# Layer B's products of 128 columns in its first two groups as one product of whole F32 operands

## The chip, the cores and the metric

The kernel runs on one core of a Trainium2 chip. The metric is the time of one execution on the device in microseconds; a kernel's time is the median of several runs.

## The reference, cut to what matters

A decoder trunk of two layers on 1024 tokens of width 1024. Layer A is an mLSTM mixer, which the change leaves alone. Layer B is dilated sliding-window attention: 8 heads of width 128 and three groups with dilations 1, 4 and 16. In each group the tokens of one residue form a sequence that is cut into blocks of 128, and a query block sees its own block and the one before:

```python
GROUPS_B = ((128, 1), (512, 4), (2048, 16))
sc = jnp.einsum('nbqhd,nbkhd->nbhqk', qb, kb) * HEAD_DIM_B ** -0.5
sc = jnp.where(valid, sc + bias, -jnp.inf)
m = sc.max(-1)
e = jnp.exp(sc - m[..., None])
den = e.sum(-1)
o = jnp.einsum('nbhqk,nbkhd->nbqhd', e, vb) / den
```

With dilation 1 there is one sequence of eight blocks, with dilation 4 there are four of two blocks, with dilation 16 sixteen sequences of 64. A first block has no block before it, so its scores have 128 columns of keys; all others have 256. The three groups' outputs are then merged by their softmax denominators, gated, and projected.

## The kernel before

**Products in parts.** TensorE multiplies most matrices as F32R, a shorter form of F32. To keep the accuracy a matrix is held as a high and a low part (`split`: ScalarE's L92 casts to the high part, L93, mostly on VectorE, subtracts to get the low one), and `mm3` makes three products of them: high by high (L97), high by low (L98) and low by high (L99). L97 and L98 have the same stationary operand. In layer B's third group (dilation 16, `g == 2`) the scores (L1136) and the values' products (L1202) instead take whole F32 operands of 128 x 128 in one product.

**Layer B.** Heads are taken in two quads of four (`quad`), and in each quad group after group (`g` = 0, 1, 2), and in a group head after head. For each quad and group `values` first makes the values of four heads; then for each head `queries_keys` makes queries and keys by seven products of half-matrices (Strassen's scheme, `strassen_steps`, banks 0 to 3, products of 512 columns; the weights are loaded by L177, subtracted and added by L243 to L261, split at L92 and L93), `scores` makes eight score blocks with their row maxima (L1142, L1144) and exponentials (L1146), and `attend` transposes the probabilities on TensorE (L1159), splits them and multiplies them with the values (`av`).

**Blocks of 128 columns.** In `scores` of group 2 (dilation 4, `g == 1`) the even blocks, four a head, have 128 columns; in group 1 it is the first block alone. In `attend` two blocks of one key block are joined to 256 columns, and three products a head in group 1, four in group 2, are left with 128.

**Where the whole matrices come from.** `done` in `queries_keys` reads a quarter of queries (`i` = 0) or keys (`i` = 1) and writes its high part (ScalarE, L1095) and its low part (VectorE, L1096). Even blocks of group 2 lie in the quarters with `half == 0`.

**Residual blocks.** `residual(tb)`, called after each head of quad 0's second group, brings one block of 128 tokens of layer A's output up to date: a load (L989), a multiplication and an addition on VectorE (L845, L846) and a store (L991), all in slot 52.

**The order.** The program is recorded in the order of the code; a scheduler then sets the order of each engine's queue and of SP's queue, which issues all DMAs. Each queue runs strictly in that order. A slot (tile `s...`) or PSUM bank (`b...`) is written anew only after its last reader. Slots 38 and 39 hold the weights' quarters, slots 32 to 35 the four values' tiles; banks 4 and 5 take scores and transposes in turn, 6 and 7 the outputs. The values' weights of a next group land in part in two of the values' tiles of the group before.

## Time and profile before

| | |
|---|---|
| median of 3 runs | 2071.47 us (2068.67 to 2078.06) |
| the profiled execution's own time | 2070.5 us |
| its span | 2068.7 us |
| TensorE busy | 2001.8 us, 97% |
| VectorE busy | 1462.1 us, 71% |
| ScalarE busy | 1003.1 us, 48% |

Engines in the profile: PE is TensorE, PEld its loads of the stationary operand, DVE VectorE, ACT ScalarE, SP the queue that issues DMAs. Times are us, in groups the mean of one instruction is in ns. Records of TensorE overlap: a product's record lasts longer than the distance to the next one's start. A row of the timeline gives the start, the duration, the engine, the line, the operation, what it writes and reads, the shape and how many instructions the row joins; in brackets the engine's idle time before it and what ended it. A 128x512 product has 512 columns.

### The profile page before, as it was taken

The numbers are of one execution on the slowest core, as the hardware profiler recorded it, in microseconds if no ns is written. First come the engines' busy times: TensorE is split into PE (matmuls) and PEld (weight loads), VectorE is DVE, ScalarE is ACT, GpSimd is POOL, SyncE is SP. The second block draws the span as 40 slices with busy tenths as digits, with TensorE's granted clock in tenths as the row PEclk, the third lists the DMA queues.
The fourth block names the chain that finished last, engine by engine and source line by source line (L and its number), as shares of the span: only waits on it lengthen the run. The fifth ranks groups of instructions, "written<-read, shape, count | busy, mean of one in ns | idle before, by whom it ended". The sixth has DMA issues, their size and how long they took to land.

```text
span 2068.7 us, 29452 instructions
## 1 busy us (share of the span) xinstructions
PE 2001.8 (97%) x11008; PEld 1721.8 (83%) x11008; DVE 1462.1 (71%) x2825; ACT 1003.1 (48%) x1920; POOL 188.9 (9%) x145
## 2 busy tenths in 40 slices
PE   8989999999999999999999999999999999999997
PEld 6868888899888888877788898888888898888786
DVE  8787788465367767465678757766878757757878
ACT  5455555533745453343434536555534635655631
POOL 0230000600244443000000000000000000000000
PEclk9999999999999999999999999999999999999999
DMA  4455555443844643516113231122543132123753
GB/s 166 145 190 175 181 214 175 153 146 114 324 172 158 214 146 114 199 62 213 56 46 127 68 133 62 61 93 91 187 166 121 64 113 70 62 92 106 260 210 122
DMA packets 117046, 288.20 MB, mean 139 GB/s; under 512 B 13028, under 2 KB 43172, under 8 KB 116904
## 3 DMA queue, kind: packets, MB, share of 16 engines
q1 hardware_dynamic: 116904, 286.34, 39.2%
q8 instruction: 86, 1.41, 0.3%
q14 instruction: 56, 0.46, 0.1%
HBM read 200.00 MB, written 86.30 MB: 138 GB/s over the span
## 4 chain that ended last, share of the span: by engine, by line
PE 77%; DVE 11%; DMA 7%; ACT 2%; issue 2%; SPq 0%; DVEq 0%; ACTq 0%
PE b L97 24%; PE b L99 24%; PE b L98 24%; DVE s L93 3%; DMA s<-df 3%; PE b L521 1%; PE b L1159 1%; DMA s<-dv 1%; DVE s L141 1%; ACT s L92 1%; PE b L527 1%; PE b L788 1%; DVE s L1276 1%; DVE s L486 1%; DVE s L230 0%
## 5 line engine op out<-in xcount | busy, mean ns | idle before, releaser
L97 PE MATMUL b<-s,s 128*128 128x512 f32 (+2 forms) x3256 | 1125.4, 354 | 28.4 <-ACT s L92 16.7
L98 PE MATMUL b<-s,s 128*128 128x512 f32 (+2 forms) x3256 | 1140.6, 352 | 9.3 <-DVE s L93 9.3
L99 PE MATMUL b<-s,s 128*128 128x512 f32 (+2 forms) x3256 | 1125.1, 352 | 5.3 <-DVE s L93 5.1
L97 PEld LDWEIGHTS b<-s,s 128*128 128x128 f32 x3256 | 617.0, 190 | 117.4 <-ACT s L92 22.3
L92 ACT CAST s<-s 128x512 fp32r<-128x512 f32 (+4 forms) x674 | 435.1, 659 | 552.9 <-PE b L99 318.3
L98 PEld LDWEIGHTS b<-s,s 128*128 128x128 f32 x3256 | 619.7, 190 | 88.1 <-DVE s L93 10.7
L99 PEld LDWEIGHTS b<-s,s 128*128 128x128 f32 x3256 | 617.9, 190 | 88.5 <-DVE s L93 8.4
L93 DVE TENSOR_TENSOR s<-s,s 128x512 fp32r<-128x512 f32 (+3 forms) x656 | 500.9, 773 | 248.0 <-ACT s L92 245.4
L230 DVE TENSOR_TENSOR s<-s,b 128x512 f32<-128x512 f32 x192 | 130.5, 682 | 70.8 <-PE b L99 61.5
L224 DVE TENSOR_TENSOR s<-s,b 128x512 f32<-128x512 f32 x128 | 86.5, 680 | 26.6 <-PE b L99 25.9
L1146 ACT ACTIVATE s<-s,nmax 128x128 f32<-128x128 f32 (+1 forms) x192 | 84.5, 442 | 38.3 <-DVE nmax L1144 37.5
L93 DVE TENSOR_TENSOR s<-b,s 128x512 fp32r<-128x512 f32 (+1 forms) x96 | 59.0, 630 | 43.3 <-ACT s L92 43.0
L486 DVE SCALAR_TENSOR_TENSOR s<-s,c_convw,s 128x512 f32<-128x512 f32 (+3 forms) x96 | 74.8, 786 | 2.3 <-ACT s L483 1.8
L1142 DVE CUSTOM_DVE_ANT_0 s<-b,k 128x128 f32<-128x128 f32 (+1 forms) x192 | 57.8, 345 | 17.5 <-PE b L99 17.4
L243 DVE TENSOR_TENSOR s<-s,s 128x512 f32<-128x512 f32 (+1 forms) x55 | 41.6, 756 | 39.3 <-DMA s<-in_w_xm 13.9
L722 ACT ACTIVATE s<-s,k 128x128 f32<-128x128 f32 x144 | 46.9, 392 | 41.7 <-DVE s L93 19.3
L92 ACT CAST s<-b 128x512 fp32r<-128x512 f32 (+1 forms) x96 | 50.3, 545 | 31.8 <-PE b L99 19.7
L681 POOL TENSOR_TENSOR s<-s 128x512 fp32r<-128x512 f32 x32 | 43.3, 1369 | 161.6 <-DMA s<-dv 112.4
L93 POOL TENSOR_TENSOR s<-s,s 128x512 fp32r<-128x512 f32 x18 | 30.5, 1702 | 254.1 <-ACT s L92 253.2
L237 ACT COPY s<-b 128x512 f32<-128x512 f32 x64 | 37.4, 585 | 26.0 <-PE b L99 25.6
L792 POOL TENSOR_TENSOR s<-s,s 128x512 f32<-128x512 f32 x32 | 42.3, 1338 | 62.8 <-DVE s L791 47.9
L1095 ACT ACTIVATE s<-s 128x512 fp32r<-128x512 f32 x48 | 42.0, 882 | 11.8 <-DVE s L230 11.6
(178 smaller groups left out, 1448.4 us busy)
## 6 DMA issues: line engine op xcount, KB each, us to landing
s<-in_w_qk SPq DMA_DIRECT2D x48, 512.0 KB
s<-in_w_out SPq DMA_DIRECT2D x40, 512.0 KB
dp<-s SPq DMA_DIRECT2D x32, 512.0 KB
s<-dp SPq DMA_DIRECT2D x32, 512.0 KB
s<-in_w_z SPq DMA_DIRECT2D x24, 512.0 KB
s<-in_w_v SPq DMA_DIRECT2D x24, 512.0 KB
dg<-s SPq DMA_DIRECT2D x24, 512.0 KB
s<-dg SPq DMA_DIRECT2D x24, 512.0 KB
```

The lines of the kernel that those rows point to most:

```text
L92: self.nc.scalar.copy(h, src)
L93: (l_eng or self.nc.vector).tensor_tensor(l, src, f(h), op=ALU.subtract)
L97: mm(ps, lh, rh, start=start, stop=False, skip_group_check=skip)
L98: mm(ps, lh, rl, start=False, stop=False, skip_group_check=skip)
L99: mm(ps, ll, rh, start=False, stop=stop, skip_group_check=skip)
L224: V.tensor_tensor(o, p, q, op=add)
L230: V.tensor_tensor(o, p[lane][rows], q[lane][rows], op=add)
L486: V.scalar_tensor_tensor(u[i][:, lo:o + 512], xm[i][:, lo - s:o + 512 - s], convw[:, c, 3 - s:4 - s], u[i][:, lo:o + 512], op0=ALU.mult, o ...
L681: G.tensor_tensor(l, f(l), f(h), op=ALU.subtract)
L722: A.activation(E[:, i * P:i * P + P], src[:, i * P:i * P + P], AF.Exp, bias=self.bias[:, hd, ig, j:j + 1])
L1142: V.tensor_tensor_reduce(out=dst, in0=sc, in1=bias, op0=ALU.add, op1=ALU.max, scale=1.0, scalar=-3e38, accum_out=mx[:, b:b + 1])
L1146: A.activation(res[b][0], res[b][0], AF.Exp, bias=nm[:, b:b + 1], accum_out=stat[:, 1, g, b:b + 1])
```

## The change

In group 2 the four even blocks' scores, and in groups 1 and 2 the values' products of 128 columns, take whole F32 operands in one product.

- `queries_keys` in group 2 writes whole queries and keys of the even blocks into a new tile in slot 52 (L1099 of the new file). The queries of these blocks are no longer split, since nothing else reads them; the keys are split as well, since the odd blocks read them.
- `transposed` splits only the columns that 256-column products read; the rest of its bank goes to a new small tile `pw` (two buffers) by one ScalarE copy (L1181).
- `head_values` also hands out the values unsplit, straight from the values' tiles, and `av_whole` (L1193) multiplies them with `pw`; the new scores line is L1145.

```diff
@@ head_values, queries_keys
-            return [(h[:, at(b)[0], at(b)[1]], l[:, at(b)[0], at(b)[1]]) for b in range(8)]
+            whole = lambda half, t: v[half][i].rearrange("p (t n) -> p t n", t=4)[:, t, cs]
+            return [(h[:, at(b)[0], at(b)[1]], l[:, at(b)[0], at(b)[1]], whole(*at(b))) for b in range(8)]
...
+            whole = self.slot(52, (P, 2, 4, P)) if g == 1 else None
...
+                if g == 1 and half == 0:
+
+                    A.activation(whole[:, i], sv, AF.Copy, scale=scale)
+                    if i == 0:
+                        return
                 A.activation(dh, sv, AF.Copy, scale=scale)
                 V.scalar_tensor_tensor(dl, sv, scale, f(dh), op0=ALU.mult, op1=ALU.subtract)
@@ scores
+                    elif g == 1 and b % 2 == 0:
+                        T.matmul(ps[:, o:o + w], whole[:, 0, b // 2], whole[:, 1, b // 2], start=True, stop=True,
+                                 skip_group_check=True)
                     else:
                         self.mm3(ps[:, o:o + w], qh[:, bs], ql[:, bs], kh[:, ks], kl[:, ks], True, True, skip=True)
@@ attend
-                    self.split(ph[:, 0:n], pl[:, 0:n], pt[:, 0:n])
+                    m = n - P * n_whole
+                    self.split(ph[:, 0:m], pl[:, 0:m], pt[:, 0:m])
+                    if n_whole:
+                        pw = self.t(cp, [P, 2, P], tag="pw", bufs=2)
+                        A.copy(pw[:, 0:n_whole].rearrange("p j n -> p (j n)"), pt[:, m:n])
+                        return ph, pl, pw
...
+            def av_whole(bank, o, kb, p2, j, start):
+
+                T.matmul(po[bank][:, o:o + P], v[kb][2], p2[2][:, j], start=start, stop=True,
+                         skip_group_check=True)
...
-                    p2 = transposed(q0, q1[:, 0:P], q1[:, P:256])
+                    p2 = transposed(q0, q1[:, 0:P], q1[:, P:256], n_whole=1)
                     at = 256 * (r % 2)
-                    av(r // 2, at, 256, 2 * r, p2, 0, r % 2 == 0)
-                    av(r // 2, at + P, P, 2 * r + 1, p2, 256, False)
+                    av(r // 2, at, 2 * r, p2, 0, r % 2 == 0)
+                    av_whole(r // 2, at + P, 2 * r + 1, p2, 0, False)
```

The change also moves instructions, since the scheduler orders the new program anew. TensorE, where head 0's last outputs of group 2 (`b_1761`, in the new file `b_1770`) meet head 1's first scores (`b_1794`, `b_1808`). Before:

```order
L97 MATMUL b_1761_11368<-s_1769_11412,s_1758_11361 128x256
L98 MATMUL b_1761_11368<-s_1769_11412,s_1758_11361 128x256
L99 MATMUL b_1761_11368<-s_1769_11412,s_1759_11362 128x256
L97 MATMUL b_1761_11368<-s_1769_11412,s_1758_11361 128x128
L98 MATMUL b_1761_11368<-s_1769_11412,s_1758_11361 128x128
L99 MATMUL b_1761_11368<-s_1769_11412,s_1759_11362 128x128
L97 MATMUL b_1794_11571<-s_1773_11431,s_1772_11430 128x128
L98 MATMUL b_1794_11571<-s_1775_11433,s_1772_11430 128x128
L99 MATMUL b_1794_11571<-s_1773_11431,s_1774_11432 128x128
L97 MATMUL b_1794_11571<-s_1773_11431,s_1772_11430 128x256
```

and now (`pw` the copied probabilities, `s_1789` the whole queries and keys in slot 52):

```order
L1193 MATMUL b_1770_11353<-pw_11387,s_1736_11100 128x128
L97 MATMUL b_1770_11353<-s_1781_11397,s_1767_11346 128x256
L1145 MATMUL b_1808_11557<-s_1789_11419 128x128
L98 MATMUL b_1770_11353<-s_1781_11397,s_1767_11346 128x256
L99 MATMUL b_1770_11353<-s_1781_11397,s_1768_11347 128x256
L1193 MATMUL b_1770_11353<-pw_11400,s_1736_11100 128x128
L97 MATMUL b_1808_11557<-s_1786_11416,s_1785_11415 128x256
```

Each run of three 128-column products is one product there, and whole products stand between parts of 256 columns. SP's queue, at the start of quad 0's first group, where head 1's weights of queries and keys (`in_w_qk`) are issued (`dx` is the stored output of layer A, `dz` a gate). Before:

```order
L989 DMA s_1771_11425<-dx_77_142 128x1024
L1307 DMA dz_89_154<-s_1484_9208 128x512
L991 DMA dx_77_142<-s_1771_11425 128x1024
L989 DMA s_1811_11683<-dx_78_143 128x1024
L177 DMA s_1587_9973<-in_w_qk 128x1024
L177 DMA s_1588_9975<-in_w_qk 128x1024
L991 DMA dx_78_143<-s_1811_11683 128x1024
```

and now:

```order
L1329 DMA dz_89_154<-s_1484_9208 128x512
L177 DMA s_1589_9971<-in_w_qk 128x1024
L177 DMA s_1590_9973<-in_w_qk 128x1024
L177 DMA s_1630_10228<-in_w_qk 128x1024
L177 DMA s_1631_10230<-in_w_qk 128x1024
```

The residual blocks' loads and stores have left this place. They stand now in the second group, here after head 0's scores there (SP's queue; `s_1784` and `s_1829` are slot 52, `s_1835` and `s_1836` head 2's weights, `s_1881` and `s_1880` head 3's):

```order
L177 DMA s_1835_11671<-in_w_qk 128x1024
L989 DMA s_1784_11410<-dx_77_142 128x1024
L177 DMA s_1836_11673<-in_w_qk 128x1024
L991 DMA dx_77_142<-s_1784_11410 128x1024
L1234 DMA dg_84_149<-s_1783_11406 128x1024
L989 DMA s_1829_11661<-dx_78_143 128x1024
L177 DMA s_1881_11924<-in_w_qk 128x1024
```

One residual block follows each head's scores, and the next head's whole queries and keys can be written only after its store. On ScalarE the write (L1099) stands now among these:

```order
L92 CAST s_1778_11384<-b_1777_11380 128x256
L1099 ACTIVATE s_1789_11419<-b_1792_11424 128x512
L1232 COPY s_1783_11406<-b_1769_11352 128x2x256
L1099 ACTIVATE s_1789_11419<-s_1796_11428 128x512
L1102 ACTIVATE s_1786_11416<-s_1796_11428 128x4x128
L92 CAST s_1781_11397<-b_1780_11393 128x256
L1181 COPY pw_11387<-b_1777_11380 128x128
```

The first L1099 there is the one that waits for the residual block's store; what is below it in the list waits with it.

## Rows read from the trace of the kernel before

**Rows 1.** The page: busy time of each engine; the chain's share by engine.

```profile
PE 2001.8 (97%) x11008; PEld 1721.8 (83%) x11008; DVE 1462.1 (71%) x2825; ACT 1003.1 (48%) x1920; POOL 188.9 (9%) x145
...
PE 77%; DVE 11%; DMA 7%; ACT 2%; issue 2%; SPq 0%; DVEq 0%; ACTq 0%
```

**Rows 2.** Busy time by stretch: length, then PE, PEld, DVE, ACT, POOL; clock, DMA.

```profile
1295.00:1322.00 27.00, 27.00 (x150) 23.34 (x149) 20.77 (x49) 16.67 (x36) 0.00 (x0) 1.00 0.16 59
```

**Rows 3.** Groups by line and shape, layer B: count, busy us, mean ns, idle before.

```profile
L99 PE MATMUL b<-s,s 128*128 128x128 f32 x96 | 25.9, 274 | 0.0
...
L1136 PE MATMUL b<-s,s 128*128 128x128 f32 x128 | 17.0, 290 | 2.0 <-ACT s L1091 2.0
L1202 PE MATMUL b<-s,s 128*128 128x128 f32 x128 | 16.8, 274 | 0.0
```

**Rows 4.** Timeline of PE: scores of a head of group 2.

```profile
1341.75 0.22 PE L97 MATMUL b<-s,s 128*128 128x128 f32 x1
1341.81 0.28 PE L98 MATMUL b<-s,s 128*128 128x128 f32 x1
1341.92 0.27 PE L99 MATMUL b<-s,s 128*128 128x128 f32 x1
1342.03 0.33 PE L97 MATMUL b<-s,s 128*128 128x256 f32 x1
...
1342.43 0.22 PE L97 MATMUL b<-s,s 128*128 128x128 f32 x1
...
1343.01 0.52 PE L99 MATMUL b<-s,s 128*128 128x256 f32 x2
```

**Rows 5.** Timeline of PE: a run of 256-column parts; whole products of group 3.

```profile
1185.26 0.28 PE L98 MATMUL b<-s,s 128*128 128x256 f32 x1
...
1186.94 0.22 PE L97 MATMUL b<-s,s 128*128 128x128 f32 x1
...
1417.77 0.39 PE L97 MATMUL b<-s,s 128*128 128x512 f32 x1
1418.00 1.95 PE L1136 MATMUL b<-s,s 128*128 128x128 f32 x16
...
1420.01 0.40 PE L99 MATMUL b<-s,s 128*128 128x512 f32 x1
```

**Rows 6.** Timeline of SP, DVE and PE: first heads of quad 0's first group.

```profile
1085.30 0.32 SPq L991 DMA_DIRECT2D dx<-s  x1
1087.98 0.32 SPq L989 DMA_DIRECT2D s<-dx  x1
1088.40 1.82 SPq L177 DMA_DIRECT2D s<-in_w_qk  x2
...
1091.48 1.22 DVE L845 TENSOR_TENSOR s<-s,s 128x1024 f32<-128x1024 f32 x1 [1.62 <-DMA s<-dx]
...
1092.96 0.39 PE L99 MATMUL b<-s,s 128*128 128x512 f32 x1
1094.06 0.50 PE L97 MATMUL b<-s,s 128*128 128x512 f32 x1 [0.71 <-ACT s L92]
1094.40 0.40 PE L98 MATMUL b<-s,s 128*128 128x512 f32 x1
1095.76 0.50 PE L97 MATMUL b<-s,s 128*128 128x512 f32 x1 [0.96 <-DVE s L230]
...
1149.03 0.50 PE L97 MATMUL b<-s,s 128*128 128x512 f32 x1 [1.22 <-DVE s L1096]
```

**Rows 7.** The chain in order of time: start, length, what.

```profile
1089.89 4.43 DMA s<-in_w_qk
```

**Rows 8.** Groups by line and shape, layer B's ACT and DVE: mean ns after busy us.

```profile
L1091 ACT ACTIVATE s<-s 128x512 f32<-128x512 f32 x24 | 28.9, 1205 | 22.8 <-DVE s L230 22.2
L92 ACT CAST s<-b 128x384 fp32r<-128x384 f32 x40 | 18.5, 494 | 1.9 <-PE b L1159 1.8
...
L929 ACT ACTIVATE s<-b,c_lnT 128x128 f32<-128x128 f32 x6 | 2.6, 466 | 0.0
...
L1096 DVE SCALAR_TENSOR_TENSOR s<-b,s 128x512 fp32r<-128x512 f32 x16 | 11.0, 685 | 2.9 <-ACT s L1095 2.9
```

More of the change, by code (lines that the diff above doesn't have):

```diff
@@ L1099, in queries_keys @@
             self.strassen(self.quarters(a["w_qk"][g, h]), x, ones, None, done, V)
-            return [(None, th[i], tl[i]) for i in range(2)]
+            return [(whole, th[i], tl[i]) for i in range(2)]
         def table(h, g):
@@ L1111, in scores @@
         def scores(h, g, qk, stat):
-            (_, qh, ql), (_, kh, kl) = qk
+            (whole, qh, ql), (_, kh, kl) = qk
             tb = table(h, g)
@@ L1153, in attend, with transposed @@
                 whole = [self.slot(14, (P, 2, 512)), 0]
-            def transposed(*parts):
+            def transposed(*parts, n_whole=0):
                 pt = self.bank(pS)
@@ L1165, in transposed, with av @@
                     ph, pl = self.pair(pts)
-                    self.split(ph[:, 0:n], pl[:, 0:n], pt[:, 0:n])
+                    m = n - P * n_whole
[4 more added lines that the diff above has]
+                        return ph, pl, pw
                 return ph, pl
-            def av(bank, o, w, kb, p2, at, start):
-                (vh, vl), (ph, pl) = v[kb], p2
-                self.mm3(po[bank][:, o:o + w], vh, vl, ph[:, at:at + w], pl[:, at:at + w],
+            def av(bank, o, kb, p2, at, start):
+                (vh, vl, _), (ph, pl) = v[kb], p2[0:2]
+                self.mm3(po[bank][:, o:o + 256], vh, vl, ph[:, at:at + 256], pl[:, at:at + 256],
                          start, True, skip=True)
+            def av_whole(bank, o, kb, p2, j, start):
+                T.matmul(po[bank][:, o:o + P], v[kb][2], p2[2][:, j], start=start, stop=True,
+                         skip_group_check=True)
             if g == 0:
@@ L1180, in attend @@
                         parts.append(sp[b + 2][:, 0:P])
-                    p2 = transposed(*parts)
+                    p2 = transposed(*parts, n_whole={1: 2, 3: 1}.get(b2, 0))
                     bank = b // 4
-                    av(bank, (b % 4) * P, 256, b, p2, 0, b == 0)
+                    av(bank, (b % 4) * P, b, p2, 0, b == 0)
                     if b2 == 1:
-                        av(0, 384, P, 3, p2, 256, False)
-                        av(1, 0, P, 3, p2, 384, True)
+                        av_whole(0, 384, 3, p2, 0, False)
+                        av_whole(1, 0, 3, p2, 1, True)
                     elif b2 == 3:
-                        av(1, 384, P, 7, p2, 256, False)
+                        av_whole(1, 384, 7, p2, 0, False)
                     else:
-                        av(bank, (b % 4) * P + P, 256, b + 1, p2, 256, False)
+                        av(bank, (b % 4) * P + P, b + 1, p2, 256, False)
             elif g == 1:
```

## Prediction

> **What bounds the kernel now.** I read the page's engine rows first, then the chain, then the stretches of layer B, then single products. TensorE is busy for 97% of the span and carries 77% of the chain that ends last; VectorE has 71%, ScalarE 48% [rows 1]. A mean over stages can mislead, so I look at the stretch that the change sits in: over one head of the second group (dilation 4, 1295 to 1322 us) TensorE is busy for 27.00 of 27.00 us, VectorE for 20.77 and ScalarE for 16.67 [rows 2]. So in the heads TensorE is the bound, without gaps, and time that is taken from its stream comes off the end, as long as the two other engines keep ahead. TensorE waits only in a few places; two of them, 1093 and 1095 us, matter here [rows 6].
>
> A busy time of TensorE is no price: a 128-column product has records of 0.22 to 0.28 us that overlap. I price by the distance from one start to the next.
>
> **The three-part product of 128 columns.** Such a product is L97, L98, L99 with 128 columns. In the scores of one head the starts are 1341.75, 1341.81, 1341.92, and the next product begins at 1342.03 [rows 4]. The first step is 0.06 us (L97 and L98 hold the same stationary part), the second and third are 0.11: there the stationary part changes. The 0.28 us up to 1342.03 are not all of it, since the following 256-column product is slowed in its first step. From 1341.75 to 1343.01 there stand two 128-column products and five 256-column parts. A 256-column part takes 0.12 us (14 steps from 1185.26 to 1186.94) [rows 5], so two products take 1.26 − 5 × 0.12 = 0.66 us, **0.33 us each**.
>
> **The whole product.** Group 3 already multiplies whole F32 operands of 128 × 128. One product of the program shows as two records: 64 products, x128 [rows 3]. From the 512-column part at 1417.77 to the one at 1420.01 there are 16 records, eight products, and two 512-column parts of 0.23 us: (2.24 − 0.46) / 8 = **0.22 us each** [rows 5]. It is the same shape, type and engine as the added product, and the neighbours are parts of the same kind, so I take it as the price.
>
> **How many.** Scores of group 2: 4 of a head; the values' products: 3 of a head in group 1, 4 in group 2. 11 × 8 heads = 88 products. (Of the 96 in [rows 3] the eight first blocks of group 1 stay in three parts.) Gain: 88 × (0.33 − 0.223) = **9.4 us**, all in stretches where TensorE has no gap. Bounds: if only the 0.28 us up to the next start were won back, 88 × 0.06 = 5 us; with 0.22 for the whole product 88 × 0.11 = 9.7 us. I take 9.4, since the stretched first step of the follower belongs to the three parts.
>
> [...]
>
> **What the residual blocks do.** The new tile of whole queries and keys lies in slot 52, which the residual blocks 4 to 7 (load of x1, two VectorE instructions, store) also use. So these move: before, they stand on SP's queue ahead of head 1's weights; now each stands behind the scores of a group-2 head. Before, that place costs something: the store at 1085.30 holds slot 52 till the load at 1087.98, and head 1's weights are issued only behind it at 1088.40; VectorE then waits 1.62 us for the load at 1091.48 [rows 6], and the chain runs through these weights for 4.43 us [rows 7]. TensorE's steps at 1092.96 and 1094.40 are 1.10 and 1.36 us instead of 0.23: 2.0 us lost [rows 6]. With the residuals gone from there I take these **2.0 us** as won; bounds 0 (the weights come late for another reason) and 2.0. A third wait, 1.22 us before 1149.03 behind VectorE [rows 6], I don't count; if the new order removes it as well, that much more is won.
>
> In their new place each of four group-2 heads gets one load, two VectorE instructions of 1.22 us and one store. VectorE has 27 − 20.8 = 6.2 us free in such a head [rows 2], so 2.4 us fit, the more so as each such head loses one subtraction of 0.69 us [rows 8] and four smaller ones shrink. On SP's queue both weight loads of the head after next stand ahead of the store, so they don't wait for it. What does wait is ScalarE: the write of the next head's whole queries (L1099) waits for the store, and behind it in ScalarE's order stand the conversions of queries and keys, the copy of the outputs and the copies of probabilities that TensorE needs. From the last whole score of a head the chain is load 3.5 us (1087.98 to 1091.48), VectorE 2.4 to 4.5 us with what stands between the two instructions, store 2.7 us (1085.30 to 1087.98): 8.6 to 10.7 us [rows 6]. In TensorE's new order there stand, till the next strassen needs the bank that L1099 frees, 51 parts of 512 columns, seven of 256, two whole products and twelve transposes (a record of 0.11 each, as a whole product's): 51 × 0.23 + 7 × 0.12 + 2 × 0.22 + 12 × 0.11, some 14 us. So the wait is covered with 3 to 5 us to spare: cost 0.
>
> **The rest.** ScalarE gains one strided conversion (1.2 us at most, by the like one of group 3 in L1091) and four copies (0.47 us at most each, by the dearest 128-column instruction that reads PSUM, L929) in a head of group 2, two copies in one of group 1, while the casts of 0.49 us at 384 columns shrink [rows 8]; 16.7 + 3.1 of 27 us stays below TensorE. The last values' product of a step now waits for subtraction and copy one after the other; other strassen parts stand before it in TensorE's order. The value tiles live until TensorE has read them whole, so the next group's weights, which land in two of them, wait for TensorE; in the order that is the second head's last product, over a head before they are used. All three: 0, hidden behind TensorE's own stream; if that cover fails, some tenths of a us in each of the 16 heads, some 3 us.
>
> **Sum.** The profiled execution took 2070.5 us, 1.8 more than its span of 2068.7. 2070.5 − 9.4 − 2.0 = 2059.1 us. It lay 1.0 under the median of the runs, 2071.5, so against that median I forecast 2060.1 us, 0.55% less. A measurement of this kernel can tell about 0.5% (10.4 us) from no change, and the forecast lies just past that.
>
> **Rivals.**
> 1. *Most of the gain comes, part is given back.* The order is new in all of layer B's heads; the waits at 1093 and 1095 us come back elsewhere, or whole products that stand alone between 256-column parts gain only the 0.06 us. For it: VectorE has only 6 us of 27 free there, so a wait in its fixed order is soon TensorE's [rows 2]. Against it: heads without any gap before [rows 2]. Time: between 2071.5 − 5 = 2066 and 2071.5 − 9.4 = 2062, so within 0.5%. Chance 0.36.
> 2. *Only columns count.* Were each of three parts 0.06 us, as the step with the stationary part kept, a product would take 0.18 us and the change would cost 88 × 0.04 = 3.5 us; with the 2.0 won, 2073. [...] Against it: the steps of 0.11 us in [rows 4]. Chance 0.03.
> 3. *Slower: the turn in slot 52 is not covered.* Three of the four residual blocks are followed by another write of whole queries. If store and load are late on SP's queue, ScalarE stands still with the casts of the next strassen behind it, and TensorE runs dry. Uncovered, each turn costs up to 10.7 us: 2071.5 − 11.4 + 32 = 2092. It decides from the point where a store lands more than 14 us behind the last whole score; to be slower than before by 0.5%, more than 7 us beyond it. Against it: the chain's 8.6 to 10.7 us. Chance 0.05.
> 4. *The change doesn't do what it says*, the whole products cost much more in accumulation with three-part neighbours than alone. At 0.33 us nothing is won but the 2.0: 2069.5. Against it: the eight products in [rows 5] stand among such parts. Chance 0.03.
>
> **How the numbers follow.** The forecast has 0.53, and with it faster by over 0.5%. Within 0.5%: rivals 1, 2 and 4, 0.42. Slower by over 0.5%: rival 3, 0.05. The range leaves out rivals 2, 3 and 4: upward to 5 us of gain and one of cover lost, 2067.5; downward the forecast less the third wait, the upper price of 9.7 and some 3 us by which medians of a few runs differ (2068.7 to 2078.1 before): 2055.
>
> **What would show it.** Right: 112 records of the values' new line and 64 of the scores' new line (two a product); eight each left of L97, L98, L99 at 128 columns in layer B; whole products spaced by 0.11 us a record; no gap at 1093 to 1096; group-2 heads about 1 us shorter with TensorE still busy throughout. Wrong: starts spaced wider than 0.11 us around whole products (price), a wait of ScalarE at L1099 on a store of x1 with a gap of TensorE behind it (rival 3), or gaps scattered in the heads behind ScalarE's copies (rival 1).

## The result and the profile after

The changed kernel takes 2061.9 us (median of 7 runs, 2059.0 to 2068.3), the kernel before beside it 2073.8 us (7 runs). The ratio is 0.995, with a 95% interval of 0.9936 to 0.9963. In a second comparison (below, e11) it is 0.995 again, 0.9934 to 0.9965. That is some 10 us of 2075, faster by the least that a measurement of this kernel tells from no change; the forecast was 0.55%.

The profiled execution has a span of 2060.2 us, 8.6 less than the one before. The page, busy time of each engine and the chain's share by engine, to be read beside [rows 1]:

```profile
PE 1994.1 (97%) x10920; PEld 1714.0 (83%) x10920; DVE 1449.3 (70%) x2817; ACT 1014.7 (49%) x1976; POOL 188.8 (9%) x145
...
PE 75%; DVE 11%; DMA 8%; ACT 3%; issue 2%; SPq 0%; DVEq 0%; ACTq 0%
```

TensorE is still the bound. In stretches of the changed kernel (columns as in [rows 2]), a head of the second group and the place of the old waits at 1093 and 1095 us [rows 6]:

```profile
1303.00:1329.00 26.00, 26.00 (x142) 22.37 (x141) 21.18 (x52) 17.83 (x42) 0.00 (x0) 1.00 0.28 101
1085.00:1100.00 15.00, 15.00 (x68) 12.43 (x67) 10.47 (x16) 6.29 (x11) 0.00 (x0) 1.00 0.19 71
```

Both are full. The groups of layer B by line and shape, as [rows 3]: the values' whole products (two records each), the whole scores, and what is left of L99 at 128 columns:

```profile
L1193 PE MATMUL b<-pw,s 128*128 128x128 f32 x112 | 20.3, 274 | 0.0
...
L1145 PE MATMUL b<-s 128*128 128x128 f32 x64 | 12.0, 273 | 0.0
...
L99 PE MATMUL b<-s,s 128*128 128x128 f32 x8 | 2.2, 273 | 0.0
```

So the change does what it says: 112 + 64 records are 88 products, and 88 of 96 three-part products are gone. The timeline of TensorE in a head's scores shows the new price, against [rows 4]:

```profile
1332.57 0.38 PE L1145 MATMUL b<-s 128*128 128x128 f32 x2
1332.71 0.36 PE L97 MATMUL b<-s,s 128*128 128x256 f32 x1
1332.91 0.28 PE L98 MATMUL b<-s,s 128*128 128x256 f32 x1
1333.03 0.28 PE L99 MATMUL b<-s,s 128*128 128x256 f32 x1
1333.15 0.38 PE L1145 MATMUL b<-s 128*128 128x128 f32 x2
```

From one whole product to the next there are 0.58 us with three parts of 256 columns between; less 3 x 0.12 that leaves 0.22 us. The starts alone would say 0.14 (1332.57 to 1332.71): the missing 0.08 sits in the follower's first step, 0.20 instead of 0.12. The same stretching was counted for the three parts.

Why a product of 128 columns has this price, the loads of the stationary operand (PEld) show, which I had not read. In the kernel before, at the three-part product of [rows 4]:

```profile
1341.75 0.19 PEld L98 LDWEIGHTS b<-s,s 128*128 128x128 f32 x1
1341.86 0.19 PEld L99 LDWEIGHTS b<-s,s 128*128 128x128 f32 x1
1341.97 0.19 PEld L97 LDWEIGHTS b<-s,s 128*128 128x128 f32 x1
1342.08 0.19 PEld L98 LDWEIGHTS b<-s,s 128*128 128x128 f32 x1
```

Every record of TensorE has a load of its own (11008 of each, [rows 1]), and L98 has one too, although it holds the same stationary part as L97. At 128 columns the loads begin 0.11 us apart. A three-part product takes three such steps, a whole one with its two records two: 3 x 0.11 = 0.33 and 2 x 0.11 = 0.22. The first load lies under the product ahead, and so the last step shows only in the follower. That the loads set the step is a reading of these rows; no run varied them alone.

**Where the 8.6 us went.** All kernels here have the same 6064 products of 512 columns, in the same order of work, so the n-th of them is a milestone: its start in one trace less its start in another tells how far the one is ahead. Up to layer B's first group, some 1082 us, TensorE's instructions are the same in all kernels, and two traces may already differ there by several us; so each stage is read by what it adds. The table (q0 and q1 are the quads), worked out so from the traces, gives each stage's difference to the trace of the kernel before in us (minus is gained); quad 0 ends and quad 1 starts in the third stage.

| kernel | ahead of it | q0 group 1 | q0 group 2 | q0 group 3, turn | q1 group 1 | q1 group 2 | q1 group 3 | projection |
|---|---|---|---|---|---|---|---|---|
| forecast | 0 | -3.3 | -3.4 | 0 | -1.3 | -3.4 | 0 | 0 |
| changed, first trace | 0.3 | -5.0 | -0.2 | -1.5 | -1.6 | -3.4 | -0.3 | 3.3 |
| changed again (e11) | 5.5 | -5.0 | 0.5 | -0.5 | -1.6 | -3.4 | 1.7 | 4.7 |
| changed, end reordered (e7) | -2.9 | -5.0 | 0.8 | 3.7 | -1.6 | -3.4 | 0.8 | -0.6 |
| residuals early (e1) | -0.3 | -0.5 | -3.4 | 1.5 | -1.5 | -3.4 | 2.6 | 0.6 |
| residuals late only (e2) | -0.7 | -3.8 | 0.5 | -0.1 | 0.0 | 0.0 | 2.7 | 0.6 |
| whole scores only (e3) | 3.1 | -3.8 | 4.7 | -3.1 | 0.8 | -1.8 | 0.4 | 4.5 |
| whole values only (e4) | 0.0 | -1.0 | -1.7 | -2.1 | -1.6 | -1.7 | 0.4 | 1.5 |
| the same again (e12) | 0.6 | -2.2 | -1.7 | -1.9 | -1.6 | -1.7 | 1.5 | -0.3 |
| whole scores twice (e5) | 2.7 | -5.0 | 0.6 | 0.3 | -1.5 | 0.2 | 2.7 | 0.7 |
| three-part scores twice (e6) | 7.5 | -0.3 | 5.6 | 1.3 | 0.0 | 5.4 | 2.5 | 0.2 |
| changed, slot 13 (e9) | 3.9 | -5.0 | -2.2 | 3.9 | -1.5 | -3.4 | 2.7 | 0.7 |
| slot 13 and end (e10) | 3.1 | -5.0 | -1.1 | 0.6 | -1.3 | -3.4 | 0.7 | 1.0 |
| before, end reordered (e8) | -0.9 | -0.4 | 0.0 | 1.5 | 0.0 | 0.0 | -0.1 | 1.0 |

Three things stand out. Quad 1 has no residual blocks, and in its first two groups TensorE has no gap: there the gain is about the forecast one, 5.0 us for 44 products against 4.7. In quad 0 the first group gains more than forecast, the second nothing. And at the output projection 3.3 us are given back.

### The profile page after: what moved, and what is told of

Its sections match the earlier page's. It is cut to its first block, busy times and chain, and to the rows that moved or that the text cites. A ratio compares the mean times of both kernels' runs of the same rounds, so it can differ in the third digit from the quotient of the medians.

```text
span 2060.2 us, 29351 instructions
## 1 busy us (share of the span) xinstructions
PE 1994.1 (97%) x10920; PEld 1714.0 (83%) x10920; DVE 1449.3 (70%) x2817; ACT 1014.7 (49%) x1976; POOL 188.8 (9%) x145
## 4 chain that ended last, share of the span: by engine, by line
PE 75%; DVE 11%; DMA 8%; ACT 3%; issue 2%; SPq 0%; DVEq 0%; ACTq 0%
PE b L99 23%; PE b L97 23%; PE b L98 23%; DVE s L93 3%; DMA s<-df 3%; PE b L521 1%; PE b L1170 1%; DMA s<-dv 1%; ACT s L92 1%; DVE s L141 1%; PE b L527 1%; PE b L788 1%; DVE s L1298 1%; PE b L1193 1%; DVE s L486 1%
## 5 line engine op out<-in xcount | busy, mean ns | idle before, releaser
L97 PE MATMUL b<-s,s 128*128 128x512 f32 (+1 forms) x3168 | 1109.3, 358 | 27.2 <-ACT s L92 17.1
L98 PE MATMUL b<-s,s 128*128 128x512 f32 (+2 forms) x3168 | 1120.6, 355 | 10.6 <-DVE s L93 10.6
L99 PE MATMUL b<-s,s 128*128 128x512 f32 (+2 forms) x3168 | 1103.7, 355 | 5.7 <-DVE s L93 5.4
L92 ACT CAST s<-s 128x512 fp32r<-128x512 f32 (+4 forms) x674 | 435.6, 659 | 534.7 <-PE b L99 287.1
L97 PEld LDWEIGHTS b<-s,s 128*128 128x128 f32 x3168 | 601.7, 190 | 114.5 <-ACT s L92 23.2
L93 DVE TENSOR_TENSOR s<-s,s 128x512 fp32r<-128x512 f32 (+3 forms) x656 | 501.2, 774 | 259.8 <-ACT s L92 257.3
L98 PEld LDWEIGHTS b<-s,s 128*128 128x128 f32 x3168 | 604.0, 191 | 90.3 <-DVE s L93 12.2
L99 PEld LDWEIGHTS b<-s,s 128*128 128x128 f32 x3168 | 601.2, 190 | 89.1 <-DVE s L93 10.0
L230 DVE TENSOR_TENSOR s<-s,b 128x512 f32<-128x512 f32 x192 | 130.3, 681 | 64.9 <-PE b L99 55.7
L93 DVE TENSOR_TENSOR s<-b,s 128x512 fp32r<-128x512 f32 (+1 forms) x96 | 51.1, 552 | 38.5 <-ACT s L92 38.1
L92 ACT CAST s<-b 128x512 fp32r<-128x512 f32 (+1 forms) x96 | 43.7, 480 | 31.7 <-PE b L99 20.7
L93 POOL TENSOR_TENSOR s<-s,s 128x512 fp32r<-128x512 f32 x18 | 30.8, 1716 | 253.4 <-ACT s L92 253.3
L1103 DVE SCALAR_TENSOR_TENSOR s<-s,s 128x512 fp32r<-128x512 f32 x48 | 42.1, 883 | 14.8 <-ACT s L1102 14.5
```

The costliest lines, as they stand in the source:

```text
L92: self.nc.scalar.copy(h, src)
L93: (l_eng or self.nc.vector).tensor_tensor(l, src, f(h), op=ALU.subtract)
L97: mm(ps, lh, rh, start=start, stop=False, skip_group_check=skip)
L98: mm(ps, lh, rl, start=False, stop=False, skip_group_check=skip)
L99: mm(ps, ll, rh, start=False, stop=stop, skip_group_check=skip)
L230: V.tensor_tensor(o, p[lane][rows], q[lane][rows], op=add)
```

## The experiments

### The price of a product: e5 and e6

In the changed kernel each whole score product is issued twice (e5); in the kernel before each three-part score product of 128 columns (e6).

```diff
@@ e5, scores
                     elif g == 1 and b % 2 == 0:
+                      for _ in range(2):
                         T.matmul(ps[:, o:o + w], whole[:, 0, b // 2], whole[:, 1, b // 2], start=True, stop=True,
@@ e6, scores
+                      for _ in range(2 if g == 1 and b % 2 == 0 else 1):
                         self.mm3(ps[:, o:o + w], qh[:, bs], ql[:, bs], kh[:, ks], kl[:, ks], True, True, skip=True)
```

> The changed kernel with each of the second group's 32 whole score products issued twice (64 instead of 32; work is added, the values are the same): the price of a whole product among its neighbours. Theory: 32 x 0.22 = 7.1 us slower than the changed kernel; in quad 1's second group, where TensorE has no gap, 16 x 0.22 = 3.6 us. Rival (a whole product costs what only its columns say, 0.06 us a record): 32 x 0.12 = 3.8 us, 1.9 us in quad 1.

> The kernel before with each of the second group's 32 score products of 128 columns in three parts issued twice (work is added, the values are the same): the price of what the change removes. Theory: 32 x 0.33 = 10.6 us slower than the kernel before; in quad 1's second group 16 x 0.33 = 5.3 us. Rival A (only the distance of starts, 0.28 us): 9.0 us, 4.5 us in quad 1. Rival B (only columns count, 0.18 us): 5.8 us, 2.9 us in quad 1.

Timed, e5 is 0.9967 (0.9949 to 0.9985) and e6 1.0074 (1.0055 to 1.0093) of the kernel before. The whole times are too coarse for a price: for the 7.1 us expected between e5 and the change the two ratios give 3.5, and for the 10.6 expected between e6 and the kernel before they give 15, with an interval (11.4 to 19.3) that leaves 10.6 out. So the price is read in quad 1's second group, between two milestones of TensorE's timeline, products of 512 columns (L99) ahead of and behind the group. In the changed kernel:

```profile
1705.72 0.39 PE L99 MATMUL b<-s,s 128*128 128x512 f32 x1
...
1871.67 0.48 PE L99 MATMUL b<-s,s 128*128 128x512 f32 x1
```

in e5:

```profile
1710.81 0.39 PE L99 MATMUL b<-s,s 128*128 128x512 f32 x1
...
1880.39 0.48 PE L99 MATMUL b<-s,s 128*128 128x512 f32 x1
```

in the kernel before:

```profile
1713.77 0.39 PE L99 MATMUL b<-s,s 128*128 128x512 f32 x1
...
1883.17 0.48 PE L99 MATMUL b<-s,s 128*128 128x512 f32 x1
```

and in e6:

```profile
1727.91 0.39 PE L99 MATMUL b<-s,s 128*128 128x512 f32 x1
...
1902.68 0.48 PE L99 MATMUL b<-s,s 128*128 128x512 f32 x1
```

The stretch takes 165.95 us in the changed kernel and 169.58 in e5: 3.63 us for 16 more whole products, **0.227 us each**. In e6 it takes 174.77, against 169.40 in the kernel before: 5.37 us for 16 more three-part products, **0.336 us each**. The difference is 0.109 (forecast 0.107), and both rivals by distances of starts or by columns alone fall. A record of 128 columns costs 0.112 us in three parts and 0.113 in whole products.

The Trainium skill ("TensorE: Matmul & The Clock Gate", Back-to-back issue gap) gives 134 cycles, an estimate of 56 ns, for 128 columns as the gap of a product by itself, and says that this is too little where a load goes with every product, about 81 ns there. The trace agrees that it is too little; the measured 0.112 us decides.

### The two halves: e3, e4 and e12

e3 keeps the whole scores and puts the values' products back in three parts; e4 keeps the whole values' products and has neither whole scores nor their tile, so that the residual blocks stay where they were.

```diff
@@ e3, attend
...
-                    av_whole(r // 2, at + P, 2 * r + 1, p2, 0, False)
+                    av(r // 2, at + P, 2 * r + 1, p2, 256, False, P)
...
@@ e4, queries_keys
-            whole = self.slot(52, (P, 2, 4, P)) if g == 1 else None
+            whole = None
...
```

> The changed kernel with the values' products of 128 columns back in three parts: 32 whole products (scores of the second group) are left, and the residual blocks stay in the second group. Theory (0.107 us a product wherever it stands): slower than the changed kernel by 56 x 0.107 = 6.0 us before the output projection; of the gain there 32 x 0.107 + 2.0 = 5.4 us are left, or 6.6 with the wait at 1149 us. Heads of the first group gain nothing against the kernel before, heads of the second 0.43 us each. Rival A (a product gains only the distance of starts, 0.06 us): slower by 3.4 us. Rival B (the whole scores gain nothing, since a whole product stands alone between 256-column parts): slower than the changed kernel by all of its gain except the 2 to 3 us of the residual blocks.

> The changed kernel with the second group's scores of 128 columns back in three parts and without the tile of whole queries and keys: 56 whole products are left, and the residual blocks stand where they stood before. Theory: before the output projection the gain is 56 x 0.107 = 6.0 us, so 5.8 us less than the changed kernel's 11.8 us, of which 3.4 us are the 32 score products and 2 to 3 us the waits at 1093 to 1096 and 1149 us, which are back. Rival A (0.06 us a product): a gain of 3.4 us. Rival B (the wait of ScalarE for slot 52 is what holds the second group's heads): the second group's heads are as short as in the changed kernel, or shorter.

e3 is 0.9996 of the kernel before (0.9983 to 1.001), e4 0.9945 (0.9928 to 0.9963). By stages the price holds in both: in quad 1's second group 1.8 us for 16 score products and 1.7 for 16 values' products, and the two halves add up to the changed kernel's 3.4. e4 has 1.7 us in quad 0's second group as well. e3 however loses 4.7 us there where 1.7 should be won, so 6.4 us are given back: it has the new place of the residual blocks, e4 has not. It also loses 0.8 us in quad 1's first group, where a wait of 0.57 us is new. Rival B of e3 (whole scores gain nothing) is wrong as to the products, though the timed result looks like it.

That e4 should equal the whole change in time while it has some 4 us less in the heads was the contradiction for which both ran again on one chip.

> The kernel with the whole values' products alone once more, beside the full change on one chip. By the places of the first trace 56 x 0.107 = 6.0 us below the kernel before, ratio 0.997; by its first median 0.9945. In place, both second groups gain 16 x 0.107 = 1.7 us with no wait of TensorE in quad 0's, and the first group keeps the waits at 1093 to 1096 us.

> The changed kernel as it is, beside the one with the whole values' products alone, on one chip. Open is a disagreement: by TensorE's place in the traces the score part (32 products, and the residual blocks' move) is worth 5.8 us before the output projection, while the two medians, taken beside different runs of the kernel before, are 11.8 and 12.1 us under it, so worth nothing. If the places hold (theory): this kernel 2 to 5 us below the other, since the move's gain of 3.8 us in the first group is mostly given back in the second; if the medians hold (rival): within 1.5 us. In place, the second group of quad 0 again gains nothing (waits of TensorE of 2.5 to 3.5 us at its first two heads), quad 1's second group 3.4 us.

Medians: the changed kernel 2065.0 us (9 runs), whole values alone 2066.3 us (11 runs), the kernel before 2078.0 us (19 runs); ratios 0.995 (0.9934 to 0.9965) and 0.9955 (0.9941 to 0.9969). The 1.3 us between them are within the rival's 1.5, and the intervals overlap: no timed run shows that the whole scores and the residual blocks' move together gain anything beside the values' products. The stages show how that can be: in the four stages of groups 1 and 2 the change has -10.2 and -9.5 us against -6.0 and -7.2, so 2 to 4 us more, and in the projection it gives back 3.3 and 4.7 against 1.5 and -0.3. That this is so in the untraced runs too is not shown.

The second trace of the changed kernel has a span of 2070.7 us, 10.5 us above the first, of which 5.2 lie ahead of the first group and only 0.7 in the heads of groups 1 and 2. One trace against one trace is no measure of the total of this kernel. A stage is a better one, but not everywhere: with the same instructions the turn differs by 5.2 us (-1.5 and 3.7, the change and e7), quad 0's first group by 1.2 (e4 and e12) and its second by 1.1 (e9 and e10). In quad 1's first two groups, where TensorE has no gap, traces agree within 0.3.

### Where the residual blocks stand: e1, e2 and e9

e1 is the change with the residual blocks back in the first group. e2 is the kernel before with the residual blocks in slot 13, by which alone the scheduler moves them late. e9 is the change with slot 13, so that they don't share slot 52 with the whole queries and keys.

```diff
@@ e1, against the change
-                    if (quad, g) == (0, 1):
+                    if (quad, g) == (0, 0):
                         residual(4 + h)
@@ e2 against the kernel before, e9 against the change
-            r = self.slot(52)
+            r = self.slot(13)
```

> The changed kernel with the four residual blocks called in the first group instead of the second; all 88 whole products stay. Theory (the residual blocks' place on SP's queue is worth 2 to 3 us of its own): the waits of TensorE at 1093 to 1096 us and at about 1149 us come back, 2.0 and 1.2 us, while the waits at L1099 in the second group (0.6 us in the changed kernel) go; TensorE's place counted from the end of the program is 2 to 3 us behind the changed kernel's from 1150 us on, a total of about 2062 to 2063 on a profile of the changed kernel's 2060.2 us span. Rival A (the early waits come from something else, say the new order of the heads): no difference before 1150 us, 0 in total. Rival B (the turn in slot 52 costs more than its row of 0.6 us shows): faster than the changed kernel by 1 us or more.

> The kernel before with one edit: the residual blocks take slot 13 instead of slot 52, by which the scheduler moves them into the second group; all products stay in three parts. Theory (the sum's second term is independent of the first): the waits at 1093 to 1096 and at 1149 us are gone or smaller, 2.0 to 3.2 us less than the kernel before up to 1150 us, and nothing more is gained from there to the output projection: about 0.998 of the kernel before. Rival (the waits were lost by the whole products' shorter heads, not by SP's queue): they stay, 1.000.

> The changed kernel with one edit: the residual blocks take slot 13 instead of slot 52, so that the whole queries and keys of the second group no longer wait for their stores; on SP's queue each then stands behind the next head's weights and the outputs' store, still outside the first group. Theory (the 2.5 us of waits of TensorE in quad 0's second group, at 1264 and 1293 us, come from the residual blocks standing among the heads' splits and weights): these waits go, and the gain of the first group (2.1 us at 1095 us, 1.2 us and more at 1149 us) stays, so 2 to 3 us less than the changed kernel from 1370 us on, ratio to the kernel before about 0.994. Rival (the whole products themselves bring these waits, by their new order): they stay, and this kernel is the changed one within 0.5 us before the output projection.

Timed: e1 0.9955 (0.993 to 0.998), e2 0.9991 (0.9978 to 1.0003), e9 0.9937 (0.9924 to 0.9951). What TensorE waited for between 1075 and 1250 us in e1 (us in total, times, longest), with the blocks early and all whole products:

```profile
PE b L97 <- DVE s L230: 1.7, 1, 1.7
PE b L97 <- ACT s L92: 0.7, 1, 0.7
```

These are the waits of [rows 6], and e2 has neither; it gains 3.8 us in the first group without a single whole product. In e1's trace the granted clock is also at half from the end of the second wait on, which it is not in the kernel before (columns as in [rows 2]):

```profile
1096.20:1099.30 3.10, 3.10 (x7) 2.46 (x8) 2.99 (x5) 0.56 (x1) 0.00 (x0) 0.50 0.52 168
```

It stays so for 3.4 us, some 1.6 us lost (a 512-column product takes 0.43 us instead of 0.23), and that is part of e1's -0.5. The same happens in e4 and not in e12, and about accounts for their -1.0 and -2.2.

So the first group's waits come from the blocks' place on SP's queue. The third wait of [rows 6] goes with them in e2, while e1 doesn't have it either, nor e4: whole products alone remove it too. I had expected e1 to lose 3.2 us of waits in the first group and to end 2 to 3 us behind the change; by stages it loses 4.5 there and wins 3.2 in the second group, by time the two can't be told apart.

What that costs in the second group: e1, where the blocks are gone from there, has no wait of TensorE between 1255 and 1400 us and the full -3.4 us. The changed kernel has three in that stretch, 1.9 us. Counted from start to start, as the products are priced, they cost 2.5 us; the other 0.7 of the 3.2 us lost is not traced.

```profile
PE b L98 <- DVE s L93: 0.8, 1, 0.8
PE b L97 <- ACT s L1099: 0.6, 1, 0.6
PE b L97 <- ACT s L92: 0.5, 1, 0.5
```

The first one, on VectorE's timeline (in brackets the idle time before, and what ended it):

```profile
1259.80 1.23 DVE L845 TENSOR_TENSOR s<-s,s 128x1024 f32<-128x1024 f32 x1 [0.79 <-DMA s<-dx]
...
1263.14 1.21 DVE L846 TENSOR_TENSOR s<-s,s 128x1024 f32<-128x1024 f32 x1
1264.27 0.68 DVE L247 TENSOR_TENSOR s<-s 128x512 f32<-128x512 f32 x1
1264.88 0.74 DVE L93 TENSOR_TENSOR s<-b,s 128x256 fp32r<-128x256 f32 x2
```

and on TensorE's:

```profile
1264.26 0.28 PE L97 MATMUL b<-s,s 128*128 128x256 f32 x1
1265.34 0.39 PE L98 MATMUL b<-s,s 128*128 128x256 f32 x1 [0.80 <-DVE s L93]
```

VectorE stands 0.79 us for the residual block's load and then spends 2.4 us on its two instructions; the split L93 of the last probabilities is behind them in its fixed order and comes late, by 0.80 us for TensorE. The other two begin on SP's queue:

```profile
1279.24 0.32 SPq L989 DMA_DIRECT2D s<-dx  x1
1285.03 1.26 SPq L177 DMA_DIRECT2D s<-in_w_qk  x2
1287.10 0.33 SPq L991 DMA_DIRECT2D dx<-s  x1
```

ScalarE, which needs these weights:

```profile
1291.12 0.63 ACT L92 CAST s<-s 128x512 fp32r<-128x512 f32 x1 [2.88 <-DMA s<-in_w_qk]
...
1294.29 0.61 ACT L1099 ACTIVATE s<-b 128x512 f32<-128x512 f32 x1
```

and TensorE behind it:

```profile
1293.94 0.38 PE L97 MATMUL b<-s,s 128*128 128x256 f32 x1 [0.50 <-ACT s L92]
1294.96 0.50 PE L97 MATMUL b<-s,s 128*128 128x512 f32 x1 [0.63 <-ACT s L1099]
```

In e9 one of the two weights is issued at 1278.79 and the other at 1284.55; in the change both stand behind the residual block's load and go out together from 1285.03, the one that could go earlier second. ScalarE and VectorE wait for them, and what stands behind in ScalarE's order, the cast L92 and L1099, is late for TensorE. L1099 itself does not wait for the store of the residual block (`dx`) in this trace. In e3 it does, 2.8 us in two waits, and there both weights stand behind the store too, issued from 1291.42; whether that is all of why e3 gives back twice what the change does stays open.

e9 confirms the place: TensorE's three waits are gone (0.15 and 0.35 us are left at other places), and 2.2 us are won in the second group instead of 0.2; why 1.2 of the 3.4 are still missing is open. (e10, with the same slot, wins 1.1; there TensorE waits once, 1.25 us, for VectorE's L230.) In e5 the waits don't appear either, although the blocks share slot 52 with the whole queries and keys: there the scheduler has put one of the two weights ahead of the residual block's load (1280.36 and 1284.90). So it is the order on the queues that costs, and sharing the slot need not. The timed ratio of e9 is lower than the change's by 0.0013, less than either interval.

### The end: e7, e8 and e10

What gave back 3.3 us at the projection? In the changed kernel's first trace, on SP's queue, VectorE and TensorE:

```profile
1982.50 1.58 SPq L1406 DMA_DIRECT2D s<-dx  x2
1984.18 1.33 SPq L1294 DMA_DIRECT2D s<-df  x3
```

```profile
1990.85 2.54 DVE L1311 TENSOR_TENSOR s<-s,s 128x512 f32<-128x512 f32 x4 [3.82 <-DMA s<-df]
```

```profile
1998.36 0.52 PE L97 MATMUL b<-s,s 128*128 128x512 f32 x1 [1.93 <-ACT s L92]
...
1999.53 0.63 PE L98 MATMUL b<-s,s 128*128 128x512 f32 x1
1999.96 0.63 PE L97 MATMUL b<-s,s 128*128 128x512 f32 x1
```

and by stretch (columns as in [rows 2]; the last but two is the granted clock):

```profile
1998.60:2002.10 3.50, 3.50 (x10) 2.67 (x10) 1.04 (x2) 0.26 (x1) 0.00 (x0) 0.52 0.00 0
2002.10:2008.00 5.90, 5.90 (x27) 4.87 (x26) 3.83 (x7) 0.00 (x0) 0.00 (x0) 1.00 0.00 0
```

The last heads' combination on VectorE waits 3.82 us for `df`, is then TensorE's last supplier, and TensorE waits 1.93 us for it (0.28 us at this place in the trace before). (`df` holds the factors by which a head's three groups are merged; the expectations call them gates.) From these rows I took VectorE's wait, for loads issued behind two dx loads, as the cause. Behind the wait the granted clock is 0.5, the level of 1.2 GHz, for 3.4 us, and a product of 512 columns takes 0.43 us instead of 0.23. So about half of the 3.3 us is the wait and half the clock. e7 (on the change), e8 (on the kernel before) and e10 (on e9) issue the dx loads and those of the last norm's parameters, which are needed later, behind the df loads (the place of the norm's parameters is left out of the cut).

```diff
@@ combine
-                nc.sync.dma_start(fb, self.dram["f", h][g:g + 1, :].to_broadcast([P, SEQ]))
+                self.df_load = nc.sync.dma_start(fb, self.dram["f", h][g:g + 1, :].to_broadcast([P, SEQ]))
@@ begin
-            nc.sync.dma_start(r, self.dram["x1", tb])
+            with self.tc.issue_after(self.df_load.ins):
+                nc.sync.dma_start(r, self.dram["x1", tb])
...
```

> The changed kernel with the end's edit alone: the loads of dx and of the last norm's parameters are issued behind the last df loads. Theory (what gives back 3.2 us of the changed kernel's gain at the end is the combination of heads 6 and 7 on VectorE, which waits 3.8 us for df loads issued behind two dx loads): VectorE's wait for df falls from 3.8 us to 2.5 us or less, TensorE's wait before the output projection from 1.9 us to under 1 us, and the half clock behind it goes; 1 to 3 us less than the changed kernel. Rival (the df loads take 6.7 us whatever stands ahead of them, as their 6.05 us at the head before suggest): nothing changes, within 0.5 us of the changed kernel in place.

> The kernel before with the end's edit alone. Theory (in the kernel before TensorE reaches the output projection later, so the combination of the last head is hardly late there, 0.28 us): 0 to 0.5 us less, ratio 1.000. Rival (the end of the program is bound by these loads in both kernels): 1 to 3 us less, as in the changed kernel, and then the changed kernel's end was not given back by the change.

> The changed kernel with the residual blocks in slot 13 and, at the end of layer B, the loads of dx and of the last norm's parameters issued on SP's queue behind the last gates' loads (df) of the heads' combination instead of ahead of them. Theory: both losses of the changed kernel go, 2 to 3 us in quad 0's second group and up to 3.2 us at the start of the output projection (the wait of 1.9 us for the last head's combination, and the 3.4 us at half the granted clock behind it): 14 to 17 us less than the kernel before, ratio 0.992 to 0.993. Rival A (the last gates' loads are late for another reason than the two dx loads ahead of them): the wait before the output projection stays, ratio 0.994 as with slot 13 alone. Rival B (the output projection then waits for the dx loads that were moved back): slower than with slot 13 alone.

Timed: e7 0.9939 (0.9926 to 0.9953), e8 0.9989 (0.9977 to 1.0), e10 0.9938 (0.9925 to 0.9951). e7's queue and VectorE:

```profile
1988.42 1.27 SPq L1294 DMA_DIRECT2D s<-df  x3
1989.79 2.30 SPq L1408 DMA_DIRECT2D s<-dx  x4
```

```profile
1992.77 1.29 DVE L1311 TENSOR_TENSOR s<-s,s 128x512 f32<-128x512 f32 x2 [5.17 <-DMA s<-df]
```

From issue to use the factors now take 4.4 us instead of 6.7 (4.3 in e10, 6.8 in e9 and e11 without the edit): in these two traces they land some 2.4 us sooner without the dx loads ahead of them. In e8 only the first of them do, after 3.9 us; VectorE waits a second time, 1.19 us, till 6.35 us after the first issue. And VectorE's wait is longer, not under 2.5 us as I expected, since its order changed too and, against TensorE's stream, it comes to the wait 3.6 us earlier. In e7 TensorE then has no wait at the projection and no half clock, -0.6 us instead of 3.3. In e10 and e8, 1.0 us are lost: their df store goes out later (1995.6 us in e8, 1991.4 in the kernel before), which takes away what the shorter landing gives. e10 is not faster than e9, as its rival A said, so the sum of 14 to 17 us that I had put on it is wrong.

Nor is VectorE's wait for these factors what sets the changed kernel apart. The kernel before has it as well, behind the same two dx loads, and there TensorE waits only 0.28 us:

```profile
2001.01 2.54 DVE L1289 TENSOR_TENSOR s<-s,s 128x512 f32<-128x512 f32 x4 [3.98 <-DMA s<-df]
```

What differs lies some 20 us earlier: VectorE waits for factors of an earlier head, in the changed kernel's first trace and in e11:

```profile
1970.68 1.22 DVE L1298 TENSOR_TENSOR s<-s,s 128x1024 f32<-128x1024 f32 x1 [1.73 <-DMA s<-df]
```

```profile
1981.11 1.23 DVE L1298 TENSOR_TENSOR s<-s,s 128x1024 f32<-128x1024 f32 x1 [3.08 <-DMA s<-df]
```

In the trace of the kernel before it does not wait there. The store of the last head's factors goes out later against TensorE's stream by as much (1.8 and 3.2 us), and with it all that follows. So it is in every trace with the end's old order (us):

| kernel | VectorE's wait there | the last store of factors later by | TensorE's wait at the projection | given back |
|---|---|---|---|---|
| before | 0 | 0 | 0.3 | 0 |
| e12 | 0 | 0.1 | 0 | -0.3 |
| e6 | 0 | 0 | 0.5 | 0.2 |
| e5 | 0.2 | 0.3 | 1.0 | 0.7 |
| e2 | 0.2 | 0.3 | 0.9 | 0.6 |
| e9 | 0.7 | 0.7 | 1.0 | 0.7 |
| e4 | 1.2 | 1.3 | 1.8 | 1.5 |
| e1 | 1.2 | 1.3 | 0.9 | 0.6 |
| changed, first trace | 1.7 | 1.8 | 1.9 | 3.3 |
| e3 | 2.5 | 2.6 | 3.2 | 4.5 |
| changed again (e11) | 3.1 | 3.2 | 3.4 | 4.7 |

That earlier load is issued at the same place of TensorE's stream in all of them; from its issue to its use pass 4.3 us in the kernel before, 6.1 in the first trace and 7.4 in e11. With all whole products e1, e9 and e5 give back only 0.6 to 0.7, so the change need not cost 3 us here. Why that load takes longer in one trace than in another stays open, and no run varied it alone.

## Why the prediction was right, and which steps were not

The time came out as forecast (11.9 us by the first medians, 0.5% in both comparisons, for 11.4). The price of the products, the larger term, is right in size. The second term was put together wrongly, it has a counterpart that I had set to nothing, and that the total agrees so well is in part luck: the traces show less than forecast, and for the values' products alone the same prices give 6.0 us, while their medians lie 12.1 and 11.7 us under the kernel before (e4, e12).

1. *The price*: right, and right in size. 0.336 against 0.33, 0.227 against 0.22, the difference 0.109 against 0.107. Pricing from start to start, and counting the follower's stretched first step, was the step that mattered: the 0.28 us up to the next start would have given half. My reason for the steps was wrong: I put 0.11 us down to a change of the stationary part and 0.06 to its staying. L98 has a load like the others, and the short step after L97 stands against the longer first step of the follower; each of the three loads costs 0.11. The price does not suffer, since it was taken over the whole run of products.
2. *The count* of 88 products: right. In quad 1, 5.0 us for 44 products, forecast 4.7.
3. *The waits at 1093 to 1096 us, 2.0 us*: right in cause and place, too small in size. The blocks' move alone gains 3.8 us in the first group (e2), since the wait of 1.2 us at 1149 us, which I had left out, goes as well; with 12 products of 0.107 that is the 5.0 us measured.
4. *The residual blocks' new place, cost 0*: wrong, and this is the step that failed: work put into free time of VectorE was taken to cost nothing. It costs 3.2 us in the first trace and 3.9 and 4.2 in e11 and e7 (a gain of 3.4 forecast, -0.2, 0.5 and 0.8 measured), so all that the move gains. I had argued from 6.2 us of free time of VectorE in a head. Free time is a sum over a head; the two instructions and the wait for their load stand in one place of a fixed order, ahead of the split that TensorE needs next. And I had looked at which store waits behind which weights on SP's queue, but not at the order of the two weights between them.
5. *Rival 3's turn in slot 52*: the mechanism is there, at a fraction of the price. L1099 waits for the store only in e3; in the change it is the weights that hold ScalarE, and the cover of 14 us was enough for the store.
6. *The rest, cost 0*: right where it can be read: quad 1 has the same copies and casts, and its first two groups gain in full.
7. *What is late next at the end*: a step that is missing. I had let the gain of the heads come off the end without looking at the output projection, which starts on the last head's combination; 3.3 and 4.7 us were given back there in the two traces of the change as it is. By the table above this follows how soon one load of factors lands, and varies from trace to trace.

In the heads of groups 1 and 2 the two traces of the change and e7's, which differs from it only at the end, show -10.2, -9.5 and -9.3 us for a forecast of -11.4. So rival 1 (a part is given back in new waits) describes the traces, and the forecast the median. That the medians are as low as they are is not fully explained: the trace before is one of a run of 2070.5 us, while medians of that kernel were 2073.8 to 2078.0 us.

## What to carry to other kernels

Price a product with its follower's first step in it, and test the price by issuing it twice in a stretch where the engine has no gap. A free share of an engine tells nothing about work put into one place of its fixed order: look at what stands behind it there, and who waits for that. Where traces of one program differ by more than the effect, compare them stage by stage at the same instructions, take several traces of a stage that has waits, and leave the total to medians. Before you put a loss down to a wait, look whether the kernel before has the same wait without the loss.

## What the runs showed of the hardware

- TensorE's same instructions up to layer B's first group took from 2.9 us less to 7.5 us more than in the trace before, in thirteen other traces.
- A wait of TensorE can cost about twice its length. After 1.93 us (first trace), 3.16 us (e3) and 3.42 us (e11) at the projection the granted clock went to 0.5 (1.2 GHz) for 3.4 us, and a 512-column product took 0.43 us instead of 0.23; after 1.78 us there (e4) it did not. In quad 0's first group it went to 0.5 after two waits of 0.71 and 1.69 us (e1) or 0.71 and 1.10 us (e4), and not after 0.71 and 1.54 us (e12). At the turn between the quads it fell with waits of 2.50 us (e10), 3.88 (e9) and 4.07 (e7), and not with 2.63 (e11), 3.05 (e8) and 3.43 (e1). The length of the wait alone doesn't tell.
- Each record of TensorE has a load of its own, also where the stationary operand stays the same; at 128 columns the loads begin 0.11 us apart, and a record costs 0.112 us (e6, three parts) or 0.113 us (e5, whole).
- From issue to use the same load of factors (`df`), at the same place of the queue, took from 4.3 us (kernel before, where VectorE did not wait for it) to 7.4 us (e11).
- A whole F32 product of 128 x 128 costs 0.227 us with three-part neighbours, as much as among its own kind [rows 5], and less than the three parts' 0.336.
